# A decoder step's convolution taken off GpSimd: prompt taps on VectorE, the sample's taps as one product and one sum

## The chip, the cores and the metric

The kernel runs on one core of a Trainium2 chip. The metric is the device time of one execution in microseconds, given as the median of several runs; lower is better. Engines are called PE (matrix products), DVE (VectorE), ACT (ScalarE), POOL (GpSimd) and SP (SyncE, which issues the transfers here).

## What is computed

One step of a decoder layer for 256 new prompt tokens and 8 sequences of 8 sample tokens: 320 token columns in all. Everything is float32.

```python
x1 = layer_norm(ALPHA * x + 0.5 * swiglu_ffn(x, ffn1_w1, ffn1_w3, ffn1_w2), ln1_g, ln1_b)
proj = x1 @ w_in
q, k, v, o, ig, fg, glu_a, glu_b, gate_a, gate_b = jnp.split(proj, SPLIT_IDX, axis=-1)
h_a, (C_new, n_new, m_new) = mlstm_branch(q, k, v, o, ig, fg, ...)
h_b, conv_new = conv_branch(glu_a, glu_b, conv_buf, conv_w, conv_b, conv_ln_g, conv_ln_b)
mix = (sigmoid(gate_a) * h_a + sigmoid(gate_b) * h_b) @ w_out
x2 = layer_norm(ALPHA * x1 + mix, ln2_g, ln2_b)
y = layer_norm(ALPHA * x2 + 0.5 * swiglu_ffn(x2, ffn2_w1, ffn2_w3, ffn2_w2), ln3_g, ln3_b)

def conv_branch(a, g, buf, conv_w, conv_b, ln_g, ln_b):
    u = a * sigmoid(g)
    upad = concatenate([buf, u], axis=1)          # buf: the last 30 inputs
    y = depthwise_conv(upad, conv_w) + conv_b     # 31 taps, 2048 channels
    return silu(layer_norm(y, ln_g, ln_b)), upad[:, -30:]
```

The model width is 2048 (16 tiles of 128 features), d_ff is 5632 (44 tiles), and there are 4 heads with 256 features for q and k and 512 for v.

## The kernel before

Features lie on the 128 partitions, the 320 token columns along them: 256 of the prompt, then 64 of the sample. Weights come as blocks of 128 x 128 in the order of use. Four blocks are split at a time into a high part by ACT (`whi`, L146) and a low part by DVE (`wlo`, L147), both of a reduced float32 format that PE takes at a higher rate; each block is then three matmuls (L211 to L213). The splits are issued three parts of four blocks ahead of their use (`AHEAD = 3`); each kind of part has five buffers.

The stages follow each other: the first FFN, the product with `w_in` (112 tiles of 128 output features, 16 blocks each), the product with `w_out`, the second FFN. `Norm` runs along with the end of each. It shifts the tiles by the mean of the first half of them (`center`, `_shift`), sums them and their squares, and `scaled` makes the normalised tiles at the start of the next stage, while the first products run on operands made ahead (`first_group`). In the norms around the FFNs and `w_out` (`own` is true for them), POOL does the 16 shifts of each and three in four of the subtractions in `scaled` (L988, L1077); in the convolution's norm DVE does them.

All work beside the products with weights is written as generators in four lanes. After every four blocks, `tick` advances each lane by one step, up to the next `yield`. Lane 0 has the gates and the heads (57 steps each), lane 1 the norms' tiles, lanes 2 and 3 the convolution's even and odd channel tiles. `drain` advances given lanes at once until a condition holds. This gives the order of issue. The framework then places instructions in each engine's queue by this order as a priority and by a model of when each becomes ready, so an engine's queue may differ from the order of the text.

`w_in_schedule` lists the 112 tiles. The convolution's input tiles come as pairs `a`, `g`; behind each pair stand some of the "others" (q, k, v of the heads, and o, ga of heads 0 and 1, which need the head's result). The tail has o, ga of head 2, the sixteen `gb` (which need the convolution's normalised result; L921 drains lanes 2, 3 and 1 until it is there) and o, ga of head 3.

A convolution tile (`conv`) begins when its `g` is done: a sigmoid of `g` by ACT (tanh, L246) and DVE (L251), two products that make the prompt's and the sample's inputs `pu` and `us`, tap 0 on ACT, then one tap per step. Even tiles do a tap as two DVE instructions (L620), one for the 256 prompt columns and one for the 64 of the sample. Odd tiles do it as two ACT instructions into a buffer (L616) and one POOL addition over 320 columns (L617). A tile takes 33 steps.

Of the kernel before, what the change touches and what calls it, by code (L numbers as in the profile page):

```python
# [14 lines left out]
P = 128  # L15
# [9 lines left out]
H = 4  # L25
# [12 lines left out]
# m-tiles of w_in without its gate columns  # L38
# [4 lines left out]
def w_in_schedule():  # L43
    """Groups of m-tiles of w_in in the order in which they are computed."""
# [8 lines left out]
    others = qkv(0) + qkv(1) + oga(0) + qkv(2) + oga(1) + qkv(3)  # L53
# [8 lines left out]
    tail = oga(2) + [("gb", j) for j in range(KD)] + oga(3)  # L62
# [6 lines left out]
def ffn_schedule():  # L69
    """(kind, [m-tiles]) in order: up-projections of a quarter of d_ff, then its down-projection."""  # L70
    out = []
    for q in range(NQ):
        f0 = q * QH
        rest = list(range(f0, f0 + QH))
        if q == 0:
            out.append(("up", q, rest[:2]))
            rest = rest[2:]
        out += [("up", q, [f]) for f in rest]
        out += [("down", q, [m]) for m in range(KD)]
    return out  # L80
# [6 lines left out]
def block_order():  # L87
    """The 128 x 128 blocks (matrix, k, m) of the weights in the order in which they are used."""
# [25 lines left out]
class Stream:  # L114
    """The weights' blocks in order, each as two float32r parts whose sum is the float32 block."""
# [53 lines left out]
class Kernel:  # L169
# [7 lines left out]
    # ---- work that is put between the blocks of the large products  # L177
# [20 lines left out]
    # ---- small helpers  # L198
# [16 lines left out]
    def gemm(self, accs, xs):  # L215
        """accs[m] = sum over k of block(k, m).T @ xs[k], the blocks taken in order k, m."""
# [12 lines left out]
    def scol(self, name, factor, k):  # L229
        """Column k of a vector times a factor."""  # L230
        return self.scaled[name, factor][:, k:k + 1]

    def rsqrt(self, r, v):
        """r = -2 / sqrt(v), by a step of Newton's from exp(-log(v) / 2)."""
# [8 lines left out]
    def tanh_half(self, x, bias=None):  # L243
        """tanh((x + 2 bias) / 2), which is 2 sigmoid(x + 2 bias) - 1."""
        t = self.t("th")
        self.nc.scalar.activation(t, x, AF.Tanh, scale=0.5, **({} if bias is None else {"bias": bias}))  # L246
        return t

    def sigmoid(self, x, bias=None):
        t = self.tanh_half(x, bias)  # L250
        self.nc.vector.tensor_scalar(t, t, 0.5, 0.5, op0=ALU.mult, op1=ALU.add)  # L251
        return t

    def preload_log(self):
        """The activation tables of the next norm."""
# [9 lines left out]
    def total(self, ps, n, x, start=True, stop=True):  # L265
        """ps += the sum over the partitions of x, over n."""
# [3 lines left out]
    def ahead(self, j, z, name):  # L270
        """The parts of (z g, g, b): an operand of products that the norm of z follows."""
# [9 lines left out]
    def normed(self, ps, norm):  # L281
        """The product with the normalised tiles, from that with ahead()'s."""
# [9 lines left out]
    def first_group(self, count, norm, name):  # L292
        """The first products after a norm, while its tiles are being made; both."""
# [15 lines left out]
    def joined(self, x, name):  # L309
        """hi + lo"""  # L310
# [5 lines left out]
    # ---- phases  # L316
# [34 lines left out]
    def consts(self, cp):  # L351
# [21 lines left out]
        # matrices of one and of the reciprocals of the numbers of features  # L373
# [10 lines left out]
        # gain and offset of the norms in front of products, as two parts  # L384
# [8 lines left out]
        # gains and offsets times powers of two, as the norms and the gates take them  # L393
# [8 lines left out]
        # float32r copies of constants that it holds exactly  # L402
# [5 lines left out]
    def ffn(self, n, xs, norm=None):  # L408
        """The norm of alpha x + 0.5 ffn(x); x is given, or to come from a norm."""
# [36 lines left out]
    def last_norm(self, norm):  # L446
        """The outputs, the work spread over the engines."""
# [35 lines left out]
    def affine_split(self, u, b):  # L483
        """The parts of u + b."""
# [17 lines left out]
    def gates(self, g8):  # L502
        """Per token and head: a = i - b, the running maximum and what follows from them, as rows."""
        nc, mp = self.nc, self.mp
        mm = nc.tensor.matmul
        row = lambda name: self.t(name)[:H, :]  # noqa: E731
# [3 lines left out]
        # tokens on partitions: [128, 3 token tiles, 8]  # L510
# [9 lines left out]
        # log of the sigmoid  # L520
# [28 lines left out]
        # running maximum, of the prompt and of each sequence of the sample  # L549
        seg = lambda x: x.rearrange("h (g e) -> h g e", e=NS)  # noqa: E731  # L550
# [19 lines left out]
        # weights of the sources in the new state  # L570
# [4 lines left out]
        # exp(-m_t), and exp(m_0 - M_t) of the sample  # L575
# [8 lines left out]
        # as two parts, one above the other  # L584
# [8 lines left out]
    def conv(self, i, acc_a, acc_g, done):  # L593
        """Gated input of channel tile i and its depthwise convolution."""
# [6 lines left out]
        three = lambda x: x.rearrange("p (g e) -> p g e", e=NS)  # noqa: E731  # L601
# [3 lines left out]
        srcs = lambda w: (pu[:, w:w + SEQ], us[:, :, w:w + NS])  # noqa: E731  # L605
        outs = lambda x: (x[:, :SEQ], three(x[:, SEQ:]))  # noqa: E731
        yield
        for out, src in zip(outs(y), srcs(0)):
            nc.scalar.activation(out, src, AF.Identity, scale=self.cw[:, i, 0:1], bias=self.col("conv_b", i))
        yield  # L610
        for w in range(1, CW):
            tap = self.cw[:, i, w:w + 1]
            if i % 2:
                x = mp.tile([P, T], F32, tag="tap", name="tap", bufs=2)
                for out, src in zip(outs(x), srcs(w)):
                    nc.scalar.activation(out, src, AF.Copy, scale=tap)  # L616
                nc.gpsimd.tensor_tensor(out=y, in0=y, in1=x, op=ALU.add)  # L617
            else:
                for out, src in zip(outs(y), srcs(w)):
                    nc.vector.scalar_tensor_tensor(out=out, in0=src, scalar=tap, in1=out, op0=ALU.mult, op1=ALU.add)  # L620
            yield
            if w == 3:
                nc.sync.dma_start(out=a["conv_p"][i], in_=pu[:, SEQ:])
                nc.sync.dma_start(out=a["conv_s"][i], in_=us[:, :, NS:])
        done(y)

    def twofold(self, x, inner):
        """The sample's columns x of 128 features, per sequence in four groups of columns.

        inner: low and high parts alternate; otherwise the high part comes twice first.  # L630
        """
# [8 lines left out]
    def head(self, h, q, k, v):  # L640
        """The mLSTM of head h: centred outputs (four tiles) and their scale."""
        nc, mp, a = self.nc, self.mp, self.a
        mm = nc.tensor.matmul
        seg = lambda x: x.rearrange("p (g e) -> p g e", e=NS)  # noqa: E731
# [7 lines left out]
        # rows of the gates on all partitions  # L652
# [9 lines left out]
        # decay, transposed: [source, token] of the blocks (0, 0..1), (1, 1), (sample, sample)  # L662
# [3 lines left out]
        # scores  # L666
# [19 lines left out]
        # the keys with their weights in the new state, and the new normaliser  # L686
# [13 lines left out]
        # v and the weighted keys with tokens on partitions  # L700
# [18 lines left out]
        # the query of the sample, weighted for the state  # L719
# [28 lines left out]
        # new state of the prompt  # L748
# [10 lines left out]
        # the sample's v and weighted keys with (sequence, part, token) on partitions  # L759
# [21 lines left out]
        # what the state gives to the sample, and the new state  # L781
# [34 lines left out]
        # outputs, features on partitions  # L816
# [18 lines left out]
        # the norm of the head  # L835
# [30 lines left out]
    def mixer(self, before):  # L866
        """The gated sum of the two branches and the normalised tiles."""
# [94 lines left out]
class Norm:  # L962
    """LayerNorm over the features of KD tiles [128 features, T]; add(m) when tile m is done.

    The tiles are shifted in place by the mean c of the first half of them, so that
    E[(z - c)^2] - (mu - c)^2 is at most twice the variance and loses nothing.
# [196 lines left out]
```

## Time and profile before

| | |
|---|---|
| median of 3 runs | 3026.67 us (3024.51 to 3028.08) |
| profiled execution, span from the first to the last instruction | 3020.5 us |
| PE busy in it | 2948.1 us (98%) |
| DVE, ACT, POOL busy | 1894.6, 1472.1, 422.7 us |

The profiled execution's own time is its span with what lies around it; no separate figure is recorded for it. The span stands 6.2 us under the median of the runs. In the profile, a line such as `L620 DVE SCALAR_TENSOR_TENSOR cy<-us,cw,cy` names the source line, the engine, the operation, and the tiles written and read; behind the count come busy microseconds, the mean nanoseconds of one, and the engine's idle time just before with what ended it. A line of a wait names who waited, for whom, the microseconds in total, how often, and the longest. PE's matmuls overlap in their records, so a busy PE is not always a PE at its full rate.

### The profile page before, as it was taken

How to read it: one execution, taken by the hardware profiler on the slowest of the kernel's cores; microseconds unless marked ns; L12 is line 12 of the kernel's file. 1: busy time of each engine (PE TensorE's matmuls, PEld its weight loads, DVE VectorE, ACT ScalarE, POOL GpSimd, SP SyncE). 2: the span in 40 equal slices, each digit the busy share in tenths (PEclk: the TensorE clock that was granted, in tenths of full speed). 3: DMA queues.
4: the chain of work that ended last, by engine and by line, in shares of the span. 5: the costliest groups of instructions: out<-in, count | busy, mean ns of one | idle time of the engine just before them, and what ended most of it. 6: DMA issues, size and time to landing. Idle time of an engine off the chain costs nothing.

```text
span 3020.5 us, 51247 instructions
## 1 busy us (share of the span) xinstructions
PE 2948.1 (98%) x19580; PEld 2879.5 (95%) x19580; DVE 1894.6 (63%) x3394; ACT 1472.1 (49%) x2840; POOL 422.7 (14%) x388
## 2 busy tenths in 40 slices
PE   9999999999998889999999999999999999999997
PEld 9999999999998888989889989999999999999997
DVE  5544444444459988888988886578444444444447
ACT  5434434433445666566756754445433433443444
POOL 0200000000003444032612300222100000000003
PEclk9999999999999999999999999999999999999999
DMA  6444444444443445564465454444444444444443
GB/s 223 148 151 149 150 151 148 152 147 153 148 153 114 120 134 167 169 200 147 139 200 160 152 204 139 148 137 137 153 147 153 148 149 152 148 153 147 153 148 105
DMA packets 163143, 460.37 MB, mean 152 GB/s; under 512 B 50128, under 2 KB 52944, under 8 KB 162896
## 3 DMA queue, kind: packets, MB, share of 16 engines
q1 hardware_dynamic: 162896, 457.10, 46.4%
q8 instruction: 153, 2.51, 0.3%
q14 instruction: 94, 0.77, 0.1%
HBM read 433.29 MB, written 23.74 MB: 151 GB/s over the span
## 4 chain that ended last, share of the span: by engine, by line
PE 85%; DVE 8%; ACT 2%; issue 2%; POOL 1%; DMA 1%; DVEq 0%; SPq 0%; ACTq 0%; POOLq 0%
PE acc L211 27%; PE acc L213 27%; PE acc L212 27%; DVE cy L620 3%; DVE wlo L147 2%; POOL cy L617 1%; PE ip L803 1%; PE cps L808 1%; DMA out_C_s<-c 1%; DMA c<-in_C 1%; ACT tap L616 1%; DVE z L1078 0%; ACT whi L146 0%; DVE xl L488 0%; POOL z L988 0%
## 5 line engine op out<-in xcount | busy, mean ns | idle before, releaser
L147 DVE TENSOR_TENSOR wlo<-wraw,whi 128x512 fp32r<-128x512 f32 x1568 | 1129.8, 723 | 943.2 <-ACT whi L146 938.3
L146 ACT ACTIVATE whi<-wraw 128x512 fp32r<-128x512 f32 x1568 | 982.9, 629 | 1259.8 <-PE acc L212 1179.2
L213 PE MATMUL acc<-xh,wlo 128*128 128x320 f32 x4480 | 1391.8, 312 | 19.5 <-DVE wlo L147 19.3
L212 PE MATMUL acc<-xl,whi 128*128 128x320 f32 x4480 | 1391.3, 311 | 7.0 <-DVE xl L488 7.0
L211 PE MATMUL acc<-xh,whi 128*128 128x320 f32 x4480 | 1392.6, 311 | 5.4 <-ACT whi L146 4.8
L213 PEld LDWEIGHTS acc<-xh,wlo 128*128 128x128 f32 x4480 | 844.7, 189 | 34.1 <-DVE wlo L147 26.7
L212 PEld LDWEIGHTS acc<-xl,whi 128*128 128x128 f32 x4480 | 846.9, 189 | 16.9 <-DVE xl L488 8.6
L211 PEld LDWEIGHTS acc<-xh,whi 128*128 128x128 f32 x4480 | 846.7, 189 | 14.8 <-ACT whi L146 5.3
L213 PE MATMUL acc<-hh,wlo 128*128 128x320 f32 x1408 | 434.6, 310 | 1.2 <-DVE wlo L147 1.0
L212 PE MATMUL acc<-hl,whi 128*128 128x320 f32 x1408 | 433.9, 309 | 0.0
L211 PE MATMUL acc<-hh,whi 128*128 128x320 f32 x1408 | 433.4, 309 | 0.0
L617 POOL TENSOR_TENSOR cy<-cy,tap 128x320 f32<-128x320 f32 x240 | 271.1, 1130 | 271.3 <-ACT tap L616 215.8
L988 POOL TENSOR_TENSOR z<-z,nc 128x320 f32<-128x320 f32 x48 | 53.8, 1158 | 1556.1 <-ACT nc L1011 1556.1
L213 PEld LDWEIGHTS acc<-hh,wlo 128*128 128x128 f32 x1408 | 264.2, 188 | 2.7 <-DVE wlo L147 2.7
L211 PEld LDWEIGHTS acc<-hh,whi 128*128 128x128 f32 x1408 | 264.4, 188 | 0.0
L212 PEld LDWEIGHTS acc<-hl,whi 128*128 128x128 f32 x1408 | 264.2, 188 | 0.0
L616 ACT ACTIVATE tap<-pu,cw 128x256 f32<-128x256 f32 x240 | 119.6, 502 | 39.3 <-POOL cy L617 36.1
L620 DVE SCALAR_TENSOR_TENSOR cy<-pu,cw,cy 128x256 f32<-128x256 f32 x240 | 128.9, 537 | 0.4
L313 POOL TENSOR_TENSOR z<-xh,xl 128x320 f32<-128x320 f32 x48 | 60.5, 1269 | 483.9 <-DVE h L425 234.3
L620 DVE SCALAR_TENSOR_TENSOR cy<-us,cw,cy 128x64 f32<-128x64 f32 x240 | 99.2, 413 | 0.1
L435 DVE SCALAR_TENSOR_TENSOR z<-acc,z 128x320 f32<-128x320 f32 x128 | 62.5, 488 | 52.7 <-PE acc L213 51.0
L616 ACT ACTIVATE tap<-us,cw 128x64 f32<-128x64 f32 x240 | 81.5, 340 | 13.4 <-DMA us<-in_cache 13.4
(287 smaller groups left out, 1948.0 us busy)
## 6 DMA issues: line engine op xcount, KB each, us to landing
wraw<-in_wst SPq DMA_DIRECT2D x783, 512.0 KB, 3.3
c<-in_C SPq DMA_DIRECT2D x32, 512.0 KB, 4.4
out_C_s<-c SPq DMA_DIRECT2D x32, 512.0 KB, 4.4
out_yT<-z SPq DMA_DIRECT2D x16, 160.0 KB, 1.8
out_C_p<-cn SPq DMA_DIRECT2D x4, 512.0 KB, 4.4
us<-in_cache SPq DMA_DIRECT2D x16, 120.0 KB, 4.0
out_conv_s<-us SPq DMA_DIRECT2D x16, 120.0 KB, 6.6
xraw<-in_xT SPq DMA_DIRECT2D x3, 480.0 KB, 5.5
```

The costliest lines, as they stand in the source:

```text
L146: nc.scalar.activation(hi, raw, AF.Copy)
L147: nc.vector.tensor_tensor(out=lo, in0=raw, in1=hi.bitcast(F32), op=ALU.subtract)
L211: mm(ps, hi, xh, start=first, stop=False)
L212: mm(ps, hi, xl, start=False, stop=False)
L213: mm(ps, lo, xh, start=False, stop=last)
L313: self.nc.gpsimd.tensor_tensor(out=t, in0=hi.bitcast(F32), in1=lo.bitcast(F32), op=ALU.add)
L435: nc.vector.scalar_tensor_tensor(out=z[m], in0=ps, scalar=0.5 / ALPHA, in1=z[m], op0=ALU.mult, op1=ALU.add)
L616: nc.scalar.activation(out, src, AF.Copy, scale=tap)
L617: nc.gpsimd.tensor_tensor(out=y, in0=y, in1=x, op=ALU.add)
L620: nc.vector.scalar_tensor_tensor(out=out, in0=src, scalar=tap, in1=out, op0=ALU.mult, op1=ALU.add)
L803: mm(ip[:32, :], qc[j][:, bs], x, start=j == 0 and n == 0, stop=j == 1 and n == 1)
L988: eng.tensor_tensor(out=self.z[j], in0=self.z[j], in1=self.c, op=ALU.subtract)
```

## The change

- In `conv`, every tile, odd or even, does its 30 prompt taps on DVE, one instruction each. ACT still does tap 0 of the prompt, now in the first step.
- The sample's 31 taps of a tile become, for four sequences at a time, one DVE product of overlapping windows of `us` with the taps (4 x 8 x 31 = 992 elements per partition) and one DVE sum over the innermost 31. The two halves are issued behind taps 8 and 16 as steps of their own, so that a tile takes 35 steps. ACT adds the bias at the end. The buffer `tap` (2 x 320 columns) gives way to `taps` (1 x 992).
- The second half of the sigmoid (times 0.5 plus 0.5) moves from DVE to ACT; `sigmoid` is used in `conv` and in `conv_out`.
- `_shift` and `scaled` always use DVE. POOL keeps the clearing of `pu`'s first columns, `joined` (L313), and its part of `last_norm`.
- `w_in_schedule` moves o, ga of head 2 from the tail into the others, so that 56 instead of 48 tiles are spread behind 14 pairs `a`, `g`: four behind each, where it was three or four. `gb` 0 now follows directly behind the others of the last pair.

Comments and docstrings fall away as well.

```diff
-    others = qkv(0) + qkv(1) + oga(0) + qkv(2) + oga(1) + qkv(3)
+    others = qkv(0) + qkv(1) + oga(0) + qkv(2) + oga(1) + qkv(3) + oga(2)
...
-    tail = oga(2) + [("gb", j) for j in range(KD)] + oga(3)
+    tail = [("gb", j) for j in range(KD)] + oga(3)
...
     def sigmoid(self, x, bias=None):
         t = self.tanh_half(x, bias)
-        self.nc.vector.tensor_scalar(t, t, 0.5, 0.5, op0=ALU.mult, op1=ALU.add)
+        self.nc.scalar.activation(t, t, AF.Copy, scale=0.5, bias=0.5)
...
         y = self.t("cy")
-        srcs = lambda w: (pu[:, w:w + SEQ], us[:, :, w:w + NS])
-        outs = lambda x: (x[:, :SEQ], three(x[:, SEQ:]))
-        yield
-        for out, src in zip(outs(y), srcs(0)):
-            nc.scalar.activation(out, src, AF.Identity, scale=self.cw[:, i, 0:1], bias=self.col("conv_b", i))
-        yield
+        bias = self.col("conv_b", i)
+        nc.scalar.activation(y[:, :SEQ], pu[:, :SEQ], AF.Identity, scale=self.cw[:, i, 0:1], bias=bias)
+        yield
+        yield
+        yp = y[:, :SEQ]
         for w in range(1, CW):
-            tap = self.cw[:, i, w:w + 1]
-            if i % 2:
-                x = mp.tile([P, T], F32, tag="tap", name="tap", bufs=2)
-                for out, src in zip(outs(x), srcs(w)):
-                    nc.scalar.activation(out, src, AF.Copy, scale=tap)
-                nc.gpsimd.tensor_tensor(out=y, in0=y, in1=x, op=ALU.add)
-            else:
-                for out, src in zip(outs(y), srcs(w)):
-                    nc.vector.scalar_tensor_tensor(out=out, in0=src, scalar=tap, in1=out, op0=ALU.mult, op1=ALU.add)
+            nc.vector.scalar_tensor_tensor(out=yp, in0=pu[:, w:w + SEQ], scalar=self.cw[:, i, w:w + 1], in1=yp, op0=ALU.mult, op1=ALU.add)
             yield
...
+            if w in (8, 16):
+                self.conv_sample(i, us, y, (w // 8 - 1) * NB // 2)
+                yield
+        nc.scalar.activation(y[:, SEQ:], y[:, SEQ:], AF.Identity, bias=bias)
         done(y)

+    def conv_sample(self, i, us, y, b0):
+        nc, n = self.nc, NB // 2
+        x = self.mp.tile([P, n, NS, CW], F32, tag="taps", name="taps", bufs=1)
+        src = us[:, b0:b0 + n, :]
+        (part, _), (step, _), _ = src.ap
+        win = bass.AP(src.tensor, src.offset, [[part, P], [step, n], [1, NS], [1, CW]])
+        taps = self.cw[:, i, :].unsqueeze(1).unsqueeze(1).to_broadcast([P, n, NS, CW])
+        nc.vector.tensor_tensor(out=x, in0=win, in1=taps, op=ALU.mult)
+        out = y[:, SEQ + b0 * NS:SEQ + (b0 + n) * NS].rearrange("p (g e) -> p g e", e=NS)
+        nc.vector.tensor_reduce(out=out, in_=x, axis=mybir.AxisListType.X, op=ALU.add)
...
     def _shift(self, j):
-        eng = self.nc.gpsimd if self.own else self.nc.vector
-        eng.tensor_tensor(out=self.z[j], in0=self.z[j], in1=self.c, op=ALU.subtract)
+        self.nc.vector.tensor_tensor(out=self.z[j], in0=self.z[j], in1=self.c, op=ALU.subtract)
...
-        eng = nc.gpsimd if self.own and j % 4 else nc.vector
-        eng.tensor_tensor(out=z, in0=z, in1=self.mean, op=ALU.subtract)
+        nc.vector.tensor_tensor(out=z, in0=z, in1=self.mean, op=ALU.subtract)
```

## The prediction

> **What bounds the kernel now.** I read the page's head first, then the busy times by stretch, then who PE waited for in the stretches where it was not full, and last the single operations of DVE with and without POOL beside them.
>
> ```profile
> span 3020.5 us, 51247 instructions
> ...
> PE 2948.1 (98%) x19580; PEld 2879.5 (95%) x19580; DVE 1894.6 (63%) x3394; ACT 1472.1 (49%) x2840; POOL 422.7 (14%) x388
> ```
>
> PE is the bound over the whole, and it idles for 3020.5 - 2948.1 = 72 us. DVE's 63% is a mean over stages with different limits, so I cut it up. The columns are: length, then PE, PEld, DVE, ACT and POOL busy, each with its number of instructions, then clock and DMA.
>
> ```profile
> 935.00:1000.00 65.00, 57.90 (x365) 54.14 (x364) 63.23 (x130) 37.47 (x76) 17.24 (x15) 0.92 0.43 130
> 1000.00:1110.00 110.00, 91.94 (x587) 87.32 (x587) 106.58 (x210) 74.72 (x182) 67.83 (x62) 0.97 0.40 116
> 1110.00:1400.00 290.00, 282.16 (x1745) 256.18 (x1745) 246.50 (x521) 179.09 (x399) 69.81 (x67) 0.98 0.58 176
> 1400.00:1510.00 110.00, 101.70 (x651) 96.36 (x650) 96.54 (x175) 83.58 (x211) 68.83 (x62) 0.98 0.45 134
> 1510.00:1700.00 190.00, 188.41 (x1224) 176.93 (x1223) 160.91 (x329) 130.61 (x297) 62.95 (x62) 1.00 0.56 171
> 1700.00:1942.00 242.00, 242.00 (x1575) 230.90 (x1574) 167.90 (x314) 125.28 (x235) 5.44 (x5) 0.99 0.49 166
> 1942.00:2057.00 115.00, 113.23 (x769) 112.65 (x768) 81.37 (x149) 53.23 (x96) 30.40 (x27) 1.00 0.43 145
> 2057.00:2110.00 53.00, 47.61 (x303) 45.88 (x302) 50.75 (x98) 31.62 (x63) 13.41 (x12) 0.97 0.36 121
> ```
>
> The product with w_in runs from about 935 to 1942 us. In its first 175 us PE is idle for 175 - 149.8 = 25.2 us and DVE is busy for 169.8 of 175: there DVE is the bound. From 1110 to 1942 PE idles for 17.7 us, nearly half of it (8.3) in 1400 to 1510, where POOL is densest. From 2057 to 2110, behind the next norm, it idles 5.4. Together 48 us: no more can be won in these stretches. PE's waits there, first for 935 to 1110, then the largest of 1110 to 1942, then 2057 to 2110:
>
> ```profile
> PE acc L213 <- DVE wlo L147: 11.3, 10, 1.7
> PE acc L212 <- DVE xl L488: 7.0, 4, 6.1
> PE arow L543 <- DVE acol L538: 4.7, 1, 4.7
> ...
> PE acc L213 <- DVE wlo L147: 6.4, 10, 1.7
> PE vs L765 <- DVE cat L637: 3.5, 2, 2.5
> PE ip L803 <- ACT chi L789: 3.0, 2, 1.6
> ...
> PE acc L213 <- DVE wlo L147: 5.0, 4, 3.4
> ```
>
> Nearly always the one that comes last is DVE. The chain of waits of 935 to 1110 names the work in its queue: the convolution's taps (L620), not the weights' low parts (L147).
>
> ```profile
> by line: DVE cy L620 30.8%; DVE wlo L147 13.7%; issue 8.8%; PE acc L213 8.8%; PE acc L212 8.6%; PE acc L211 8.4%; DVE z L1078 4.1%; DVE xl L488 3.3%; ACT whi L146 1.5%; DVE mrow L557 1.0%; DVE mrow L555 0.9%; ACT cy L609 0.8%; ACT L246 0.7%
> ```
>
> **What POOL costs DVE.** The groups of DVE's instructions (busy, then mean ns of one) in 1200 to 1250, where POOL is almost silent, then in 1000 to 1050, where it adds taps, then over 1000 to 1700:
>
> ```profile
> L147 DVE TENSOR_TENSOR wlo<-wraw,whi 128x512 fp32r<-128x512 f32 x18 | 12.6, 702 | 1.1 <-ACT whi L146 1.0
> L620 DVE SCALAR_TENSOR_TENSOR cy<-pu,cw,cy 128x256 f32<-128x256 f32 x23 | 11.0, 478 | 0.1
> ...
> L620 DVE SCALAR_TENSOR_TENSOR cy<-us,cw,cy 128x64 f32<-128x64 f32 x23 | 6.4, 278 | 0.0
> ...
> L620 DVE SCALAR_TENSOR_TENSOR cy<-us,cw,cy 128x64 f32<-128x64 f32 x26 | 16.5, 636 | 0.0
> L620 DVE SCALAR_TENSOR_TENSOR cy<-pu,cw,cy 128x256 f32<-128x256 f32 x26 | 15.3, 590 | 0.0
> L147 DVE TENSOR_TENSOR wlo<-wraw,whi 128x512 fp32r<-128x512 f32 x17 | 12.7, 746 | 0.0
> ...
> L559 DVE COPY mrow<-mrow 4x8 f32<-4x8 f32 x1 | 0.9, 895 | 0.0
> ...
> L147 DVE TENSOR_TENSOR wlo<-wraw,whi 128x512 fp32r<-128x512 f32 x303 | 239.6, 795 | 49.0 <-ACT whi L146 47.2 <-PE acc L212 0.8 <-PE ip L803 0.5
> L620 DVE SCALAR_TENSOR_TENSOR cy<-pu,cw,cy 128x256 f32<-128x256 f32 x236 | 127.0, 538 | 0.4
> L620 DVE SCALAR_TENSOR_TENSOR cy<-us,cw,cy 128x64 f32<-128x64 f32 x236 | 96.9, 410 | 0.1
> ```
>
> The same instruction is longer beside POOL. In 1000 to 1050 the excess of the three large groups is 26 x 0.358 + 26 x 0.112 + 17 x 0.044 = 13.0 us. About half of the 62 POOL instructions of 1000 to 1110 lie here, say 30: 0.43 us each. Smaller operations pay too (a copy of 8 elements took 0.895), so I take 0.5. Over 1000 to 1700 the three groups give 28.2 + 14.2 + 31.2 = 73.6 us for about 236 additions: 0.31 each, smaller groups left out. One instance in the timeline:
>
> ```profile
> 1000.27 4.77 POOL L617 TENSOR_TENSOR cy<-cy,tap 128x320 f32<-128x320 f32 x4
> 1000.59 0.90 DVE L620 SCALAR_TENSOR_TENSOR cy<-us,cw,cy 128x64 f32<-128x64 f32 x1
> ```
>
> A tap of 0.278 takes 0.90, which is 0.62 lost to one POOL addition. So a POOL instruction's price on DVE lies between 0.31 and 0.62; 0.5 holds for the start, where it was read. The Trainium skill (SBUF — State Buffer, Who interferes with whom) says that a DVE instruction with two SBUF inputs and a GpSimd instruction that reads SBUF exclude each other for a whole instruction. The stretched tap agrees; by that rule the upper price would hold throughout (second rival).
>
> **The new operations.** No row has the product over 992 elements (4 sequences x 8 tokens x 31 taps) or its sum. The nearest:
>
> ```profile
> L694 DVE TENSOR_REDUCE nn<-kw 128x1 f32<-128x256 f32 x8 | 3.3, 407 | 0.0
> ...
> L696 DVE TENSOR_REDUCE ns<-kw 128x8 f32<-128x64 f32 x8 | 1.6, 205 | 0.0
> ```
>
> The slope is (407 - 205) / 192 = 1.05 ns per element, so the sum takes 407 + 736 x 1.05 = 1.18 us. The product, from L147's 702 ns for 512, is 702 + 480 x 1.05 = 1.21 us. Ends: 0.70 for each (the 512-element row, did the repeated taps come cheaply), and 1.18 + 24 x 0.025 = 1.78 for the sum, if the whole 205 ns of L696 is paid by each of its 8 outputs. I take 1.21 and 1.18, since two reductions with 1 and 8 outputs lie on one line with the products. The Trainium skill (VectorE: DVE Perf Modes, Rules for kernel authors) speaks against a reduction on the hot path, calling it DVE's slowest operation; here 256 elements take 407 ns against 478 for a tap, so per element it isn't, and were it twice as long DVE would get 32 x 1.18 = 38 us more.
>
> **The change part by part.** The lanes advance once in four blocks, which is one L147 instruction: 700 / 303 = 2.31 us per step in 1000 to 1700. A w_in tile is 16 blocks, 48 matmuls of 113.23 / 769 = 0.147 us: 7.1 us of PE, and four L147, 2.8 us of DVE.
>
> *Start, 935 to 1110.* Added on DVE: some 60 prompt taps of the odd tiles (the 62 POOL instructions less memsets), 60 x 0.478 = 28.7; four tiles' samples, 4 x 2 x (1.21 + 1.18) = 19.1; 12 of the norm's subtractions over 320 elements, 0.53 each between 0.478 and 0.702: 6.4. Removed: about as many sample taps of the even tiles, 60 x 0.278 = 16.7; the stalls, (60 + 12) x 0.5 = 36. Net +1.5 us. The reordering puts four other tiles instead of three behind the convolution pairs 2 and 3: two tiles more, PE +14.2, DVE +5.6, so PE's idle time shrinks by 8.6. Start: -7.1 us, with ends of +6.6 (price 0.31, DVE +15.2) and -15.7 (price 0.62, DVE -7.1).
>
> *1110 to 1942.* Per two convolution tiles DVE gets 30 x 0.478 + 2 x 4.78 = 23.9 and loses 8.3 and 30 stalls, 9.3 to 18.6: between +6.3 and -3.0, and one further w_in tile (+7.1 PE, +2.8 DVE). DVE's share was (246.5 + 96.5 + 160.9) / 590 = 85%; per two tiles 84 of 98 us becomes 93 or 84 of 105: 89 or 80%. So it is about as full as before. At 85%, too, 1510 to 1700 lost only 1.6 us of 190, 0.8%; at that rate 590 us would lose 5 instead of 17.7. Ends 0 and -13; I take -9, nearer to the second, since that row has both the share that I expect and the steadier load.
>
> *Lanes.* A convolution takes 35 steps instead of 33. o and ga of head 2 stood between the last convolution and gb 0; they are moved ahead. gb 0 now comes 20 steps behind the last g tile, when 14 steps of convolution 15 are left, and these are issued at once: 13 x 0.478 = 6.2 us on DVE, behind it the convolution's norm. Three split parts are issued ahead, 3 x 2.31 = 6.9 us, which covers the taps but not the norm. Ends 0 and +15; I take +3. Head 3 now runs beside convolutions 13 to 15 instead of behind them: +1 (0 to +5). SP issues the same transfers; those of head 3 come earlier.
>
> *At nothing.* The sigmoid's second half moves from DVE to ACT, and the taps of odd tiles leave ACT, which was busy for at most 83.58 of 110 us; PE waits for it only 3.0 us. The 48 shifts of the norms move to DVE at the end of each FFN and of w_out, where PE hides them (113.23 of 115, DVE 81.37). If that cover is gone they cost 48 x 0.53 = 25. In 2057 to 2110, 12 subtractions (+6.4) stand against 12 stalls (-6.0): nothing, -5 to +3.
>
> Sum: -7.1 - 9 + 3 + 1 = -12.1 us. The profiled span of 3020.5 becomes 3008.4; the median of the runs shown, 3026.67, lies 6.2 above the span, so the time is 3014.6.
>
> **The rivals.**
> - *POOL's price is the full 0.62 everywhere.* For it: the stretched tap. Against it: the mean of 0.31 over 1000 to 1700. Then -15.7 - 13 + 4 = -24.7: 3002.
> - *The late end takes it back.* The convolution's norm and silu stand in front of gb 0 and cost 15, and the stretch from 1110 wins nothing: -7.1 + 15 + 1 = +9 at most, and 3027 where the burst costs 6. For it: the start of w_in waits 6.1 us at one stroke behind such a norm (L488). Against it: 1700 to 1942 loses nothing, with DVE at 69%.
> - *Slower: both lanes on DVE at once.* A lane gets a new tile every 12 w_in tiles, 48 steps, and is busy for 35 of them; the two, 24 steps apart, overlap for 22. DVE's busy time of 1000 to 1700, 106.6 + 246.5 + 96.5 + 160.9 = 610.5 us, less L147 and the taps, leaves 0.49 us per step for all else. A step with both lanes then needs 0.70 + 2 x 0.478 + 2 x 4.78 / 35 + 0.49 = 2.42 us against PE's 2.31. The excess of an overlap, 22 x 0.11 = 2.4 us, is less than the 6.9 of the parts ahead; it decides where the rest is over 0.69, as it can be in a head's state loop. At 0.8 in all seven overlaps it costs (22 x 0.42 - 6.9) x 7 = 16: -7.1 + 16 + 4 = +13, 3040. Against it: the lanes are as crowded before, 0.70 + 0.478 + 0.278 + 0.49 + up to 0.62 = 2.57, and 590 us lost 17.7.
> - *No change at all.* DVE's total does not fall (+1.5 at the start); if only that total counts, 3026.
>
> **How the numbers follow.** The forecast (3007 to 3020) has 0.47, the first rival (2994 to 3007) 0.17, the second and the fourth together (3021 to 3033) 0.14, the slower one (3033 to 3055) 0.22. A measurement here can tell about 0.2%, 6 us: faster below 3020.6, slower above 3032.7. So faster 0.64, same 0.14, slower 0.22. The range of 2994 to 3040 leaves out the tail of the slower rival, which the peaks before the change speak against; the likeliest case alone is 3007 to 3020.
>
> **What would show it.** DVE's L147 near 0.70 us all through w_in; taps at 0.478; product and sum near 1.2 us each; PE's idle time from the norm to the third convolution pair under 20 us; a wait of a few us for L147 at gb 0. It would be wrong if the sum costs 1.8 us, if PE waits for L147 grow between 1110 and the last convolution, or if PE stops for over 10 us at gb 0.

## The result, and the profile after

The changed kernel takes 2994.89 us (median of 4 runs, 2992.07 to 3001.82) against 3026.4 before (4 runs, 3024.51 to 3028.08): ratio 0.9890, 95% interval 0.9876 to 0.9905. It is 31.5 us faster; the prediction said 12. The direction was right, the size was not: the time lies 0.9 us above the low end of the range of 2994 to 3040.

The head of the page of the changed kernel:

```profile
span 2994.8 us, 50339 instructions
...
PE 2940.2 (98%) x19580; PEld 2883.3 (96%) x19580; DVE 1893.9 (63%) x3498; ACT 1340.8 (45%) x2392; POOL 70.7 (2%) x76
```

DVE's busy time is the same as before (1894.6), with 104 more instructions: what was stretched time beside POOL is now work. The span falls by 25.7 us. The other 5.8 of the 31.5 us lie in the choice of the profiled execution: the span before stands 5.9 us under its median, the span after 0.1 under its own.

The same stretches as in the prediction (length, then PE, PEld, DVE, ACT, POOL busy and instructions, clock and DMA). The product with w_in now ends 20 us earlier (w_out's first matmul starts at 1922.0 instead of 1942.2), so the last row covers a little of what follows:

```profile
935.00:1000.00 65.00, 56.44 (x369) 53.84 (x367) 60.36 (x131) 35.20 (x66) 0.00 (x0) 0.92 0.37 119
1000.00:1110.00 110.00, 106.31 (x719) 103.88 (x719) 106.10 (x244) 52.64 (x101) 0.25 (x2) 1.00 0.49 148
1110.00:1400.00 290.00, 285.67 (x1772) 262.07 (x1771) 256.19 (x520) 148.44 (x287) 0.88 (x7) 0.96 0.56 174
1400.00:1510.00 110.00, 110.00 (x713) 103.31 (x713) 103.45 (x200) 55.11 (x105) 0.25 (x2) 1.00 0.63 188
1510.00:1700.00 190.00, 190.00 (x1228) 180.41 (x1227) 167.48 (x333) 93.11 (x176) 0.37 (x3) 0.98 0.55 166
1700.00:1942.00 242.00, 229.54 (x1471) 221.57 (x1470) 163.95 (x299) 120.92 (x226) 18.33 (x16) 0.96 0.44 146
```

In the first 175 us PE's idle time fell from 25.2 to 12.3, and PE did 1088 matmuls instead of 952. DVE is as full there as before. From 1110 to 1700 the idle time fell from 17.7 to 4.3, with DVE fuller (527 instead of 504 us). The new loss is behind 1700: 12.5 us where there was none. PE's waits after the change, for 935 to 1110 and then 1110 to 1942:

```profile
PE acc L212 <- DVE xl L488: 5.7, 1, 5.7
PE acc L211 <- ACT xh L487: 2.9, 1, 2.9
PE acc L211 <- ACT th L246: 1.7, 1, 1.7
...
PE acc L211 <- ACT th L246: 7.8, 3, 4.3
PE ip L810 <- ACT chi L796: 4.3, 1, 4.3
PE mean L268 <- ACT xh L261: 3.4, 1, 3.4
PE acc L213 <- DVE wlo L147: 1.1, 1, 1.1
```

The waits for the weights' low parts, 11.3 and 6.4 us before, are down to 1.1. Apart from one wait for the norm at the start of w_in (L488), what is late now is mostly ACT: tanh (L246) empties an accumulator, and PE waits for the buffer. The chain of waits of 935 to 1110, where the taps had 30.8%:

```profile
by line: PE acc L211 27.9%; PE acc L212 27.9%; PE acc L213 27.4%; DVE z L1083 4.0%; PE acc L499 2.7%; DVE wlo L147 1.1%; PE tv L712 0.7%; DVE cy L611 0.7%; PE cp L213 0.5%; PE cp L211 0.5%; PE cp L212 0.5%; DVE parts L588 0.5%; issue 0.4%; 
```

The taps (now L611) have 0.7%. DVE's groups in 968 to 1110, before and then after:

```profile
L147 DVE TENSOR_TENSOR wlo<-wraw,whi 128x512 fp32r<-128x512 f32 x58 | 42.5, 740 | 2.6 <-ACT whi L146 2.5
L620 DVE SCALAR_TENSOR_TENSOR cy<-us,cw,cy 128x64 f32<-128x64 f32 x60 | 37.6, 627 | 0.0
L620 DVE SCALAR_TENSOR_TENSOR cy<-pu,cw,cy 128x256 f32<-128x256 f32 x60 | 35.1, 585 | 0.1
```

```profile
L611 DVE SCALAR_TENSOR_TENSOR cy<-pu,cw,cy 128x256 f32<-128x256 f32 x100 | 44.6, 473 | 0.0
L147 DVE TENSOR_TENSOR wlo<-wraw,whi 128x512 fp32r<-128x512 f32 x63 | 42.7, 680 | 3.4 <-ACT whi L146 2.9
L630 DVE TENSOR_TENSOR taps<-us,cw 128x992 f32<-128x992 f32 x8 | 9.4, 1180 | 0.0
L632 DVE TENSOR_REDUCE cy<-taps 128x32 f32<-128x992 f32 x8 | 9.4, 1172 | 0.0
```

Before, the convolution took 72.7 us of DVE here for the even tiles alone; now 63.4 us do 100 prompt taps and the samples of four tiles, and there is room for five more L147.

### The profile page after: what moved, and what is told of

The parts are those of the page before. It is cut to its first block, busy times and chain, and to the rows that moved or that the text cites. A ratio compares the mean times of both kernels' runs of the same rounds, so it can differ in the third digit from the quotient of the medians.

```text
span 2994.8 us, 50339 instructions
## 1 busy us (share of the span) xinstructions
PE 2940.2 (98%) x19580; PEld 2883.3 (96%) x19580; DVE 1893.9 (63%) x3498; ACT 1340.8 (45%) x2392; POOL 70.7 (2%) x76
## 4 chain that ended last, share of the span: by engine, by line
PE 96%; DVE 2%; DMA 1%; ACT 1%; issue 0%; DVEq 0%; SPq 0%; ACTq 0%
PE acc L211 31%; PE acc L212 31%; PE acc L213 31%; PE ip L810 1%; PE cps L815 1%; DMA out_C_s<-c 0%; PE num L836 0%; PE num L211 0%; DVE wlo L147 0%; DMA c<-in_C 0%; PE num L213 0%; PE num L212 0%; DVE z L1083 0%; DVE z L473 0%; DVE xl L488 0%; ACT th L246 0%
## 5 line engine op out<-in xcount | busy, mean ns | idle before, releaser
L147 DVE TENSOR_TENSOR wlo<-wraw,whi 128x512 fp32r<-128x512 f32 x1568 | 1080.9, 691 | 924.4 <-ACT whi L146 918.8
L611 DVE SCALAR_TENSOR_TENSOR cy<-pu,cw,cy 128x256 f32<-128x256 f32 x480 | 221.2, 476 | 1.0
L211 PE MATMUL acc<-mh,whi 128*128 128x320 f32 x256 | 79.1, 309 | 0.0
L212 PE MATMUL acc<-ml,whi 128*128 128x320 f32 x256 | 79.0, 309 | 0.0
L213 PE MATMUL acc<-mh,wlo 128*128 128x320 f32 x256 | 78.7, 309 | 0.0
L313 POOL TENSOR_TENSOR z<-xh,xl 128x320 f32<-128x320 f32 x48 | 60.7, 1272 | 632.3 <-DVE h L425 351.7
L425 DVE TENSOR_TENSOR h<-s,acc 128x320 f32<-128x320 f32 x86 | 42.0, 488 | 52.2 <-ACT s L423 52.2
L423 ACT ACTIVATE s<-acc 128x320 f32<-128x320 f32 x86 | 37.7, 438 | 69.2 <-PE acc L213 69.2
```

The costliest lines, as they stand in the source:

```text
L147: nc.vector.tensor_tensor(out=lo, in0=raw, in1=hi.bitcast(F32), op=ALU.subtract)
L211: mm(ps, hi, xh, start=first, stop=False)
L212: mm(ps, hi, xl, start=False, stop=False)
L213: mm(ps, lo, xh, start=False, stop=last)
L313: self.nc.gpsimd.tensor_tensor(out=t, in0=hi.bitcast(F32), in1=lo.bitcast(F32), op=ALU.add)
L423: nc.scalar.activation(s, accs[2 * j], AF.Silu)
```

## The experiments

Theory A, from the prediction: POOL's reads held up DVE's instructions, and the gain is that they are gone. Theory B: the gain is the order of w_in's tiles, which leaves DVE more time per convolution tile. Theory C: the gain is ACT, rid of 480 taps. Theory D, added before the runs of single parts: the norms are a main part of the gain. Each ratio is to the kernel before in the same set of runs.

**The order, undone and alone.** Undone in the changed kernel:

```diff
-    others = qkv(0) + qkv(1) + oga(0) + qkv(2) + oga(1) + qkv(3) + oga(2)
+    others = qkv(0) + qkv(1) + oga(0) + qkv(2) + oga(1) + qkv(3)
-    tail = [("gb", j) for j in range(KD)] + oga(3)
+    tail = oga(2) + [("gb", j) for j in range(KD)] + oga(3)
```

> The changed kernel with the old order of w_in tiles: o, ga of head 2 are back in the tail, ahead of gb 0, and 48 instead of 56 tiles stand between the convolution pairs; convolution and norms stay off POOL. The changed kernel took 2994.9 us against 3026.4 before. Theory A (the gain is DVE's time that POOL's reads had cost; the order gave nothing and costs the waits at gb 0, 12 us in the profile of the changed kernel): no wait at gb 0, and DVE still lighter than before, so 2985 to 2995. Theory B (the gain is the room that eight more tiles behind the convolution pairs gave to DVE): the waits for the weights' low parts come back between 1000 and 1500 us, 3005 to 3020. Theory C (ACT, rid of the odd tiles' taps, delivers the high parts and empties accumulators earlier; the order matters little): 2985 to 2997, as A.

Measured: 2993.63, ratio 0.9886 (0.9871 to 0.9901), the same as the change. The start with the old order:

```profile
1000.00:1110.00 110.00, 106.24 (x725) 104.24 (x724) 108.20 (x256) 53.44 (x103) 0.25 (x2) 1.00 0.49 149
```

PE does 725 matmuls there, with the new order 719: the two tiles more behind the first pairs, worth 8.6 us in the prediction, give nothing. With either order PE no longer waits for a low part in the first 175 us, so there is nothing for more room to win. In the kernel before, the new order alone:

> The kernel before with the new order of w_in tiles alone: taps, norms and sigmoid as before, POOL in use. Theory A (POOL's reads): nothing is won, and the convolution's end falls on gb 0, so 3022 to 3038. Theory B (room in the order): most of the gain is there, 3000 to 3012. Theory C (ACT's load): as A, 3022 to 3038.

Measured: 3022.89, ratio 0.9988 (0.9979 to 0.9997): some 4 us. Theory B falls as the main cause.

**POOL's additions beside the change, first try.** In the changed kernel, for odd tiles:

```diff
+            idle = mp.tile([P, T], F32, tag="idle", name="idle", bufs=1)
+            nc.gpsimd.memset(idle, 0.0)
...
+                nc.gpsimd.tensor_tensor(out=idle, in0=idle, in1=idle, op=ALU.add)
```

> The changed kernel with 30 additions on POOL for each odd convolution tile, 240 in all, over 128 x 320 elements of a tile of zeros that nothing else reads: POOL reads as much as before the change, and no engine waits for it. The output is not touched. Theory A: every addition stalls a DVE instruction for 0.3 to 0.6 us, 72 to 150 us more on DVE in the convolution's stretch, which is already nine tenths full, so PE waits for the low parts again: 3010 to 3035, L147 near 0.79 us there. Theories B and C: POOL's load is beside the point, under 3000.

Measured: 3000.94, ratio 0.9914 (0.9901 to 0.9928). This lies between the ranges of the theories, because the run answers another question: nothing held the additions back, so POOL did them in the first FFN, as the window shows.

```profile
0.00:935.00 935.00, 927.33 (x6304) 926.01 (x6305) 511.10 (x784) 390.68 (x667) 252.09 (x270) 1.00 0.47 155
```

There DVE is half full, its busy time rose by 42 us (469.24 in the changed kernel), and about 6 us reached the end.

**ACT's half beside the change, then ACT's and POOL's.** Here the additions are paced by ACT's taps, as before the change (the tile `idle` of the second run is made and cleared as in the first try):

```diff
+                x = mp.tile([P, T], F32, tag="tap", name="tap", bufs=2)
+                nc.scalar.activation(x[:, :SEQ], pu[:, w:w + SEQ], AF.Copy, scale=self.cw[:, i, w:w + 1])
+                nc.scalar.activation(three(x[:, SEQ:]), us[:, :, w:w + NS], AF.Copy, scale=self.cw[:, i, w:w + 1])
+                nc.gpsimd.tensor_tensor(out=idle, in0=idle, in1=x, op=ALU.add)   # second run only
```

> The changed kernel with the ACT half of the odd tiles' old way run beside it: 480 activations into a buffer that nothing reads, 201 us of ACT by the records of before. Output untouched. Theory A (POOL's reads on DVE): the waits for low parts stay away, 2993 to 3000. Theory C (ACT's load): ACT delivers high parts and empties accumulators later, 3005 to 3025.

> The changed kernel with the whole old way of the odd tiles run beside it, ACT's 480 taps and POOL's 240 additions into tiles that nothing reads; the kernel's own work waits for none of it but through the engines' queues. Output untouched. Against the same with ACT's half alone it shows POOL's reads by themselves. Theory A: 75 to 150 us of stalls on a DVE that is nine tenths full, 20 to 50 us above the run with ACT's half, 3015 to 3045. Theory C: within 5 us of the run with ACT's half.

Measured: with ACT's taps alone 2995.39, ratio 0.9887 (0.987 to 0.9905), the same as the change; with POOL's additions too 3067.03, ratio 1.0118 (1.0099 to 1.0136). Theory C falls, and 240 additions cost 0.0231 of 3026.4, 70 us, 0.29 us each: more than theory A's range, whose upper end was 3045. In the two profiles the product with w_in, where the additions are, takes 991.9 and 1060.5 us. The page and the stretch of 1000 to 1110 of the first, then of the second:

```profile
PE 2949.8 (98%) x19580; PEld 2891.5 (96%) x19580; DVE 1895.3 (63%) x3498; ACT 1483.2 (49%) x2872; POOL 71.0 (2%) x76
...
1000.00:1110.00 110.00, 107.61 (x720) 103.84 (x719) 107.02 (x247) 84.96 (x213) 0.25 (x2) 1.00 0.52 148
```

```profile
PE 2970.1 (97%) x19580; PEld 2900.8 (95%) x19580; DVE 2000.6 (65%) x3498; ACT 1487.6 (48%) x2872; POOL 361.9 (12%) x324
...
1000.00:1110.00 110.00, 95.88 (x596) 90.71 (x594) 109.08 (x197) 71.82 (x176) 61.70 (x51) 0.94 0.39 117
```

The same 3498 DVE instructions take 105.3 us longer: 0.44 us per addition. At the start PE falls from 720 to 596 matmuls, as in the kernel before (587). Theory A holds. The 0.44 is DVE's part alone; the 70 us hold all that comes with an addition. Two such things show in the profiles: the granted clock (PE's clock as a share of full speed, the column behind the busy times) is 0.94 instead of 1.00 in the stretch, and ACT waits 36 us for POOL to give a tap's buffer back. No run separates their shares.

**POOL writing instead of reading.** In place of the addition, three clearings of the tile that ACT has just written:

```diff
-                nc.gpsimd.tensor_tensor(out=idle, in0=idle, in1=x, op=ALU.add)
+                for _ in range(3):
+                    nc.gpsimd.memset(x, 0.0)
```

> The changed kernel with the ACT half of the odd tiles' old way beside it and, instead of POOL's 240 additions, 720 POOL clearings of the tile that ACT has just written (three for one addition, about as long together). POOL is as busy as with the additions but reads nothing. With ACT's half alone the ratio was 0.9887, with ACT's half and the additions 1.0118. If DVE is held up by POOL's reads: 0.987 to 0.991, taps at 0.476 us. If by any access of POOL, writes too: 1.00 to 1.015.

Measured: 2996.23, ratio 0.9895 (0.988 to 0.9911). The page, POOL's group, and DVE's two in 1000 to 1700:

```profile
PE 2942.2 (98%) x19580; PEld 2884.6 (96%) x19580; DVE 1894.2 (63%) x3498; ACT 1487.7 (50%) x2872; POOL 323.7 (11%) x796
...
L616 POOL MEMSET tap<- 128x320 f32 x720 | 252.8, 366 | 1095.0 <-ACT tap L613 997.1 <-ACT tap L614 72.5
...
L147 DVE TENSOR_TENSOR wlo<-wraw,whi 128x512 fp32r<-128x512 f32 x318 | 216.2, 684 | 34.5 <-ACT whi L146 32.0 <-PE ip L816 0.9
L617 DVE SCALAR_TENSOR_TENSOR cy<-pu,cw,cy 128x256 f32<-128x256 f32 x449 | 206.4, 476 | 0.7
```

In the run with additions the same groups are 0.800 and 0.584 long. The sample's product and sum stand below them:

```profile
L619 DVE SCALAR_TENSOR_TENSOR cy<-pu,cw,cy 128x256 f32<-128x256 f32 x406 | 229.7, 584 | 0.5
L147 DVE TENSOR_TENSOR wlo<-wraw,whi 128x512 fp32r<-128x512 f32 x283 | 225.2, 800 | 16.2 <-ACT whi L146 15.7
...
L638 DVE TENSOR_TENSOR taps<-us,cw 128x992 f32<-128x992 f32 x26 | 34.1, 1311 | 0.0
L640 DVE TENSOR_REDUCE cy<-taps 128x32 f32<-128x992 f32 x27 | 31.7, 1172 | 0.0
```

With ACT's taps alone L147, the taps, the product and the sum take 0.684, 0.476, 1.182 and 1.175 in the same stretch. So POOL busy for 324 us, most of it with writes, stretches none of DVE's groups shown, and its additions stretch the product, which reads two tiles, but not the sum, which reads one. This is what the Trainium skill states (SBUF — State Buffer, Who interferes with whom): a DVE instruction with two SBUF inputs contends with a GpSimd instruction that reads SBUF, not with one that only writes it. The Trainium skill says on the same page (SBUF: two separate sides) that whichever of the two starts first holds the port for its whole instruction. By that rule, the prediction said, its upper price of 0.62 would hold throughout; the mean here is 0.44. Some additions may meet no such DVE instruction, or be the one that waits; no run shows which.

**Which parts of the change.** Three kernels with one part each, or without one. The norms alone on DVE, in the kernel before (`_shift` and `scaled` as in the change):

> The kernel before with the norms' shifts and subtractions on DVE instead of POOL, and nothing else of the change. Theory A (POOL's reads hold DVE up by 0.3 to 0.6 us each): at the three norms DVE exchanges 72 operations of about 0.4 us for 72 stalls; PE waits there for 6.1 (start of w_in) and 3.4 us (start of the second FFN), and that is all that can be won: 3019 to 3027. Theory D (the norms' part, at places where DVE is full, is a main part of the gain): 3005 to 3018.

Measured: 3016.62, ratio 0.9966 (0.9955 to 0.9977), in the range of theory D. And undone in the changed kernel:

> The changed kernel with the norms' 48 shifts and 24 subtractions back on POOL, the rest as changed. The norms alone, moved in the kernel before, gave a ratio of 0.9966, where the sum had put nothing. If their part is real and stands by itself: the ratio rises from 0.989 to 0.992 to 0.994, 3002 to 3010, and the time is lost at the ends of the FFNs and of w_out, not within w_in. If the 0.9966 came from a new placement of w_in's work: 0.988 to 0.990, 2992 to 2997.

Measured: 3006.89, ratio 0.9930 (0.9918 to 0.9943). The norms are worth 0.34 to 0.40%, 10 to 12 us, both ways. The sample's product and sum alone, in the kernel before:

```diff
+            if i % 2:
+                x = mp.tile([P, SEQ], F32, tag="tap", name="tap", bufs=2)
+                nc.scalar.activation(x, pu[:, w:w + SEQ], AF.Copy, scale=self.cw[:, i, w:w + 1])
+                nc.gpsimd.tensor_tensor(out=yp, in0=yp, in1=x, op=ALU.add)
+            else:
+                nc.vector.scalar_tensor_tensor(out=yp, in0=pu[:, w:w + SEQ], ...)
...
+                self.conv_sample(i, us, y, (w // 8 - 1) * NB // 2)
```

> The kernel before with the sample's taps as product and sum on DVE for all tiles; odd prompt taps stay on ACT (240 activations instead of 480) and POOL (240 additions over 256 columns instead of 320); norms, order and sigmoid as before. With norms, sigmoid and order changed as well, this form took 0.992 of the time before. Theory A: the 240 short sample taps that stood behind a POOL addition are gone, POOL's reads are fewer by a fifth; DVE gets 71 us and loses 48 of its time and 33 of stalls: 3005 to 3018. Theory D (norms): 3018 to 3028, since nothing else that stands in a full place changes.

Measured: 3019.58, ratio 0.9973 (0.9964 to 0.9982). That is a little over the range of theory A and inside the other's; the norms' part and this one both exist. POOL's additions are a fifth shorter here too, and ACT has 240 taps less, so this is not the cheaper form alone. The same convolution inside the changed kernel:

> The changed kernel with the prompt taps of odd tiles back on ACT (240 activations) and POOL (240 additions over 256 columns); the sample stays with product and sum, norms and order stay as changed. DVE loses 240 taps, about 96 us of its time. Theory A with 0.3 to 0.6 us per addition: 75 to 150 us of stalls come back, DVE ends between 20 lighter and 55 heavier, 2995 to 3020, and L147 near 0.79 us again in the convolution's stretch. Theory C: ACT gets 120 us back, 3000 to 3015, L147's length beside the point. If POOL's reads cost little, DVE is 96 us lighter and this is the fastest of all: 2980 to 2990.

Measured: 3007.62, ratio 0.9919 (0.9902 to 0.9936). That lies in the ranges of theories A and C alike. The odd tiles' prompt taps are thus worth 0.9890 / 0.9919, 0.3%, little more than the two intervals allow, though DVE takes on 240 taps. Last, all taps on DVE one by one, in the kernel before:

```diff
-            if i % 2:
+            if False:
```

> The kernel before with the odd tiles' taps on DVE, done as the even ones' (two instructions per tap); no product and sum, the old order, norms still on POOL. Theory A (POOL's reads beside the taps held DVE up): DVE gets 240 x (0.478 + 0.278) = 181 us by records, some 150 us of its time, and loses the stalls of 240 additions, 75 to 150 us: no gain or a loss of up to 20 us against the kernel before, 3020 to 3045, because DVE is nine tenths full; the gain of the change then needs the cheaper sample. Theory C (ACT's 201 us of taps stood in front of high parts and of accumulators to be emptied): most of the gain is there, 2995 to 3010.

Measured: 3024.55, ratio 0.9981 (0.9971 to 0.9990). Moving the taps without the cheaper sample gives 6 us, as theory A says. Against theory C once more: this kernel has ACT as light as the change (1327.8 us busy, 1340.8 there).

The parts by single runs: norms 0.34%, sample 0.27%, odd prompt taps 0.29%, order 0.12%: 1.02% together, against 1.10% measured for all. Each has an interval of 0.1 to 0.2% to either side, so that the sum is no proof that the parts are independent; undoing the order in the changed kernel, for one, cost nothing. No part carries the change alone.

**The late end.** Half of o, ga of head 2 back ahead of gb 0:

```diff
-    others = ... + qkv(3) + oga(2)
+    others = ... + qkv(3) + oga(2)[:4]
-    tail = [("gb", j) for j in range(KD)] + oga(3)
+    tail = oga(2)[4:] + [("gb", j) for j in range(KD)] + oga(3)
```

> The changed kernel with half of o, ga of head 2 (four tiles, 16 steps) put back into the tail ahead of gb 0; gb 0 then comes 36 steps behind the last g tile, and a convolution takes 35. Theory A, with the late end as a cost of its own: the three waits of 3 to 4 us around gb 0 go, and the convolution's stretch stays free of waits for low parts: 2982 to 2989. Rival: the norm and its chain are the cost wherever they end, and the waits only move: 2992 to 2998.

Measured: 2999.8, ratio 0.9911 (0.9898 to 0.9925). This is above both ranges, and the rival's way is seen: the waits moved to the norms of head 0 (2.8 us) and head 1 (4.9 and 4.6 us near 1400) and to a wait of 5.4 us at 1818. So the distance in those norms was lengthened, by two more `yield`s ahead of each sum over partitions in `head`:

```diff
-        yield
-        yield
+        for _ in range(4):
+            yield
```

> The changed kernel with two more empty steps ahead of each of the two sums over partitions in a head's norm (a head then takes 61 steps). What remains of PE's idle time in the changed kernel are waits of 3 to 6 us for ACT, whose queue stands in such a chain. If the distance of the chain from its use is what is short: 2984 to 2991. If ACT's queue is stopped by the order in which the chain's parts are placed, wherever they are: the waits move, 2992 to 3000.

> The changed kernel with the old order of w_in tiles and the longer distances in the heads' norms: no convolution end at gb 0, no short chain. If both remove their waits: 2978 to 2988, faster than either kernel. If the waits are placed anew with every order: 2988 to 3000.

Measured: with the new order 2995.68, ratio 0.9894 (0.9880 to 0.9907), nothing; with the old order 2980.39 (4 runs, 2978.55 to 2983.01), ratio 0.9844 (0.9830 to 0.9857). This is the fastest kernel, in the range that was expected if both edits remove their waits, and its interval lies below that of the change. The waits of PE in 1110 to 1930 with the old order, then with the longer distance too:

```profile
PE acc L211 <- ACT th L246: 5.5, 2, 4.9
PE cps L815 <- ACT st L811: 3.3, 2, 2.7
PE ip L810 <- ACT chi L796: 2.7, 1, 2.7
PE acc L211 <- ACT q L916: 2.1, 1, 2.1
```

```profile
PE ip L810 <- ACT chi L796: 4.3, 1, 4.3
PE acc L213 <- DVE wlo L147: 1.0, 1, 1.0
PE cps L815 <- ACT st L811: 0.7, 1, 0.7
PE acc L211 <- ACT th L246: 0.6, 1, 0.6
```

Either edit alone leaves waits of its own. With the new order and the longer distance, PE still waits for ACT for 13.8 us between 1760 and 1830, around gb 0; with the old order alone, for 4.9 us between 1600 and 1700. The reading that the one is the convolution's end and the other the norm of a head close to its use fits these four kernels, but is argued. Why ACT's queue is late just there may be a matter of the placement by the framework's model, which was not tested.

## Why the prediction was right in direction and short in size

Taken from the first and last matmuls of each stage in the two profiles, the product with w_in became 18.6 us shorter (1006.9 and 988.3), the first FFN 1.6, the products with w_out 2.6 (115.1 and 112.5) and the first products of the second FFN 5.5 (33.8 and 28.3); 2.6 us were lost in the rest of the second FFN. That is the 25.7 us of the spans. The prediction had -12.1 for w_in and nothing elsewhere. Inside w_in, counted in matmuls of 0.147 us, the change was -20 to 1110, where it said -7.1, then -13.7 to 1700 and +15.3 to 1942, +1.6 together, where it said -5 (-9 + 3 + 1). So two steps failed: the term of the start was mis-sized by 13 us, and the norms were put at nothing.

- *The bound and the price.* That DVE's queue ended PE's waits, and that POOL's additions stretched it, was right. The price between 0.31 and 0.62 us is confirmed at 0.44, on the mean of all 240, by the two runs that differ in the additions alone.
- *The new operations* were priced at 1.21 and 1.18; the rows after have 1.18 and 1.17.
- *The start, -7.1.* This is the term that was mis-sized first: PE does 136 matmuls more in the first 175 us, 20 us of its work. Its idle time fell by 12.9 only; part of the rest is the granted clock, 0.97 in 1000 to 1110 before and 1.00 after. The split was wrong too. DVE's own exchange, put at +1.5, is the gain, since the additions put back take 124 matmuls away again; the order, put at -8.6, gives nothing there. The added work was too large in two ways: 100 prompt taps fall into the stretch instead of 120, and records overlap. Two taps in a row in the changed kernel take 0.88, not 2 x 0.478, so a further tap costs DVE 0.40:

```profile
1305.33 0.88 DVE L611 SCALAR_TENSOR_TENSOR cy<-pu,cw,cy 128x256 f32<-128x256 f32 x2
```

- *1110 to 1942, -9.* The idle time to 1700 fell by 13.4, the end that the prediction had named (-13); the late end took it back.
- *Lanes, +3 and +1.* The late end cost 12.5 us of idle time, 15.3 in matmuls, at the end of the range named (+15) and nearer to the second rival than to the +3. It did not come by the way described: not L147 behind a burst of taps, but ACT's queue. PE's longest single wait was 4.3 us, so the sign of being wrong, over 10 us at gb 0, was met in sum and not at one stroke. A wait costs more than its length here: behind the one of 4.33 us, 1788 to 1792, the granted clock was 0.58 and PE did 16 matmuls, in the next 4 us at 1.00 it did 29. At 1797 an emptied accumulator waits behind a table load and four other tanh of the same source line:

```profile
1796.24 1.28 ACT L238 ACT_TABLE_LOAD   x1
1797.53 0.47 ACT L238 ACTIVATE rs<-rsq 128x320 f32<-128x320 f32 x1
1797.91 1.90 ACT L246 ACTIVATE th<-cy,conv_ln_b_scaled 128x320 f32<-128x320 f32 x4
1799.72 0.41 ACT L246 ACTIVATE th<-acc 128x320 f32<-128x320 f32 x1
```

- *The norms, at nothing.* Wrong: 10 to 12 us, shown both ways. The prediction priced what the shifts would cost DVE and left out the stalls that POOL's shifts caused there. The cover that was named, PE busy for 113.23 of 115 us, was no proof. The end of the first FFN, 850 to 935, before, after, and after with the norms back on POOL:

```profile
850.00:935.00 85.00, 83.85 (x564) 82.34 (x564) 59.70 (x113) 41.53 (x77) 17.69 (x16) 1.00 0.39 132
```

```profile
850.00:935.00 85.00, 84.66 (x579) 84.40 (x578) 60.38 (x139) 44.70 (x83) 0.00 (x0) 1.00 0.44 146
```

```profile
850.00:935.00 85.00, 83.94 (x566) 82.43 (x564) 58.94 (x110) 41.76 (x77) 17.70 (x16) 1.00 0.42 136
```

  PE is busy for 98.6 and 99.6%, but does 564 and 579 matmuls: 15 x 0.147 = 2.2 us. So its busy share can hide lost work. What was slow is the weights' low part; L147 in 895 to 935, for the same three kernels:

```profile
L147 DVE TENSOR_TENSOR wlo<-wraw,whi 128x512 fp32r<-128x512 f32 x17 | 14.8, 873 | 4.1 <-ACT whi L146 4.1
L147 DVE TENSOR_TENSOR wlo<-wraw,whi 128x512 fp32r<-128x512 f32 x22 | 14.9, 679 | 3.3 <-ACT whi L146 3.3
L147 DVE TENSOR_TENSOR wlo<-wraw,whi 128x512 fp32r<-128x512 f32 x18 | 15.4, 863 | 4.5 <-ACT whi L146 4.4
```

  The larger part lies behind w_in. With the norms alone on DVE the products with w_out take 112.4 us and the first ones of the second FFN 28.3, as in the changed kernel (112.5 and 28.3); with the norms back on POOL 116.4 and 33.8, as before or more (115.1 and 33.8). The limit of 48 us for the whole gain was drawn from idle time alone, in stretches that leave out the end of the first FFN and w_out.
- *The sigmoid and ACT's taps, at nothing*: right for ACT's load: its 480 taps put back, 142 us more busy time, changed nothing. The sigmoid's move was not run alone.
- *The rivals.* The higher price everywhere gave 3002; the price is not the highest, yet the time is lower still, so that its nearness to the measured time is no support. The late end came, with a gain ahead of it that its rival had not. DVE's total did not fall, as the fourth has it, yet the time did. Both lanes on DVE at once cost nothing that the profile shows: from 1400 to 1700 PE does not idle at all with DVE at 90%.

## What to carry to other kernels

Where one engine's instructions are longer beside another's, price the stretched time like work that can be removed: compare the same group in a stretch with and one without the other engine, and look for it also where the bound engine seems full. Count matmuls per microsecond rather than PE's busy share when you argue that something is hidden. When a busy queue is relieved, look for the next queue in front of the accumulators: here ACT's, where an order and a distance that gave nothing alone gave 0.5% together.

## What the runs showed of the hardware

- A POOL addition of 128 x 320 float32 costs DVE 0.44 us on the mean where DVE is over nine tenths full (105.3 us for 240), and the kernel 0.29 us; where DVE is half full, it costs DVE 0.17 (42 us for 240).
- Beside these additions, in 1000 to 1700, a DVE product of two tiles grows from 1.18 to 1.31 us, a sum that reads one tile keeps its 1.17.
- POOL writes (720 clearings of 128 x 320, 0.366 each) leave L147 at 0.684 us and the taps at 0.476, as without them.
- A DVE product with an operand repeated along two dimensions and one of overlapping windows takes 1.18 us for 992 elements, and a sum over the innermost 31 of them 1.17: within 3% of what the prediction drew from the counts of elements in rows without such patterns.
- Behind a wait of PE of 4.33 us the granted clock was 0.58 over 4 us, and 1.00 over the next 4 us.
